# Two spreadings of a norm's inverse roots sent through memory, and two weight differences ordered behind a multiplication, in an encoder layer

## The chip, the cores and the metric

The kernel runs on one core of a Trainium2 chip. A core has a matrix engine (TensorE, PE in the profile; its weight loads are PEld), three engines for elementwise work (VectorE or DVE, ScalarE or ACT, GpSimd or POOL), and SyncE (SP), which here only issues DMAs. ScalarE issues DMAs too. Each engine carries out its own instructions strictly in the order in which they stand in its queue; an instruction whose operand isn't there stops everything behind it on that engine. TensorE writes to PSUM banks of 128 x 512 numbers; VectorE and ScalarE read these and the main on-chip memory (SBUF). DRAM is reached by DMA alone.

The metric is the time of one execution on the device in microseconds (us), lower is better.

## The reference

An encoder layer on 1024 tokens of width 1024, in float32. One RMSNorm feeds a projection; its columns go to two kinds of attention (A, a sliding window; B, a neighbourhood on a grid), each with 512 output columns and an RMSNorm of its own; one output projection; an RMSNorm and a gated MLP with 2816 inner columns; a last RMSNorm.

```python
def rmsnorm(x, g):
    y = x * lax.rsqrt(jnp.mean(x * x, axis=-1, keepdims=True) + EPS)
    return y * g
...
mix = jnp.concatenate([rmsnorm(o_a, norm_a[l]), rmsnorm(o_b, norm_b[l])], axis=-1)
h = h + jnp.einsum('bse,ed->bsd', mix, w_out[l])
hn = rmsnorm(h, norm_ffn[l])
h = h + conv_gated_mlp(hn, w_gate[l], w_up[l], conv_w[l], conv_b[l], w_down[l])
return rmsnorm(h, norm_final)
```

The change is in the two norms on the second and the fourth of these lines: that of attention B and that of the MLP.

## The kernel before

**Layout.** Activations lie transposed: the 128 partitions hold columns of the model, the tokens run along a row. A tile is 128 x 1024, and each is worked on in two halves of 512 tokens (h = 0 and 1). Every matrix product is made of three matmuls for each pair of blocks: operands and weights are split into a high part (ScalarE copies with rounding) and a low part (VectorE subtracts), and high x high, high x low and low x high are added up in a PSUM bank (`block`, L179 to L181, and `group`, L1043 to L1045).

**A norm.** Since a token is a column here, its sum of squares runs over partitions. `inverse_narrow` transposes the accumulated squares on TensorE (L217), VectorE reduces them to `v`, 128 partitions x 4 numbers, one for each of 512 tokens (L219), ScalarE takes the root (L220), VectorE the reciprocal (L229). These carry a high priority. `widen` then spreads `v` again: four transposes on TensorE (L236), each of one column of `v` taken 128 times, so that a PSUM bank holds each token's inverse root in all 128 partitions (tile `sw`). VectorE multiplies an activation tile by the norm's gain and by this bank in one instruction.

The second half of the last norm does it in another way (`as_rows`, L1497 and on): one transpose turns `v` into 4 rows of 128, ScalarE copies them to SBUF, a DMA writes these 2 KB to DRAM (`spread`), and a second DMA reads them back into all 128 partitions, 256 KB (`wide`). Both DMAs are issued by SyncE.

**Order.** TensorE's order is the program's own. For the other engines a planner sorts the instructions by their place in the program, their priority (`tc.high_priority`) and by when it believes their operands to be there; `behind("name")` forbids it to put what is inside ahead of a named instruction. Queues of DMAs are sorted like the engine that issues them.

**The stage.** Near 350 us the last attention units end. `vb2` holds the roots of attention B's norm for both halves. For each half the kernel spreads the root (`widen`), multiplies four tiles (L996) and splits them (L997 ScalarE, L998 VectorE) to `mg[4:8]`. Between the halves the first two output weights are begun (`load_wo`, L979 to L983) and three blocks of the A half of the output projection are run (`fill(3)`).

Then comes the B half of the output projection, for h = 0 and 1 and d = 0 to 7, four blocks of three matmuls each; every result is added to the residual (L1063), written to DRAM (`h1d`, issued by ScalarE, L1064), squared (L1067) and added up (L1069). The MLP norm's first half falls into h = 1: its `v` is made behind d = 1 and spread within d = 3, behind the second block. `normed(0, ...)` then multiplies tiles 0 to 3 and later 4 to 7 (L1074), and `operand` splits them (L1050, L1051) for the first gate products `p1` and `p2` (tiles `x` and `z`). During `p2` the second half's squares are transposed, and behind it its `v` is spread.

**The weight differences.** The gate and up products use a scheme of seven products in place of eight, which needs sums and differences of weight blocks and of operands. `head_weights(i, "s2")` makes such a difference of weights for each of the four first units (i = 0 to 3): it loads half a weight tile (L1037) and subtracts it from a sum made before (`sub`, L1083; as `ws<-ws,raw` in the profile). It stands late in the program, behind `normed(1, ...)`, but the planner can move it forward. Half tiles share three raw buffers.

Of the kernel before, what the change touches and what calls it, by code (L numbers as in the profile page):

```python
# [13 lines left out]
F32 = mybir.dt.float32  # L14
F32R = mybir.dt.float32r
AF = mybir.ActivationFunctionType
ALU = mybir.AluOpType
PSUM = bass.MemoryType.PSUM

D, S, HD = 1024, 1024, 64  # L20
KT = D // 128
NB = S // 128
HALF = 512
# [29 lines left out]
C_NMIX, C_NFFN, C_NFIN, C_NA, C_NB, C_CW, C_CB, C_SINK = 0, 8, 16, 24, 28, 32, 98, 120  # L53
# [5 lines left out]
def hybrid_layer(tc, xT, w_first, w_in, w_out, w_gate, w_up, w_down, small, sink, rpb, consts, rope, out):  # L59
    nc = tc.nc  # L60
    with ExitStack() as ctx:
# [7 lines left out]
        tpool = inner("temps", 3)  # L69
        apool = inner("att", 2)  # L70
        spool = inner("stats", 6)

        slots = {"xg": 16, "op": 14, "mix": 8, "rstd": 1}

        def big(name, tag, dt=F32):
            return lpool.tile([128, S], dt, name=name, tag=tag, bufs=slots[tag])
# [4 lines left out]
        def bank(name, tag):  # L81
            return psum.tile([128, HALF], F32, name=name, tag=tag)
# [7 lines left out]
        col = lambda c: par[:, c:c + 1]  # L90
# [15 lines left out]
        for name, dst, n in (("h", his, 2), ("h", his, 2), ("l", los, 2), ("l", los, 2), ("w", None, 2)):  # L106
            t = flat(big(name, "mix", F32R)[:, :], n)
# [26 lines left out]
        ident = cst[:, K_ID:K_ID + 128]  # L134
# [17 lines left out]
        mark = {}  # L152

        def behind(*names):

            stack = ExitStack()
            for n in names:
                stack.enter_context(tc.issue_after(mark[n].ins))
            return stack
# [51 lines left out]
        def inverse_narrow(sqs, dim, tag, n=4):  # L211

            ps = bank("ss", tag)
            v = cpool.tile([128, n], F32, name="v4", tag="v4", bufs=4, padded_shape=[128, 4])
            if len(sqs) == 1:
                for c in range(n):
                    nc.tensor.transpose(ps[:, c * 128:(c + 1) * 128], sqs[0][:, c * 128:(c + 1) * 128], ident)  # L217
                with tc.high_priority(offset=500):
                    nc.vector.tensor_reduce(v, ps[:, 0:n * 128].rearrange("p (c w) -> p c w", w=128), axis=mybir.AxisListType.X, op=ALU.add)  # L219
                    mark["narrow root"] = nc.scalar.activation(v, v, AF.Sqrt, bias=eps, scale=1.0 / dim)  # L220
            else:
                for i, sq in enumerate(sqs):
                    for c in range(n):
                        nc.tensor.matmul(ps[:, c:c + 1], sq[:, c * 128:(c + 1) * 128], ones[:, 0:1], start=c == 0 and i == 0,
                                         stop=i == len(sqs) - 1, skip_group_check=True)
                with tc.high_priority(offset=500):
                    nc.scalar.activation(v[:, 0:n], ps[:, 0:n], AF.Sqrt, bias=eps, scale=float(D) / dim)
            with tc.high_priority(offset=500):
                mark["narrow"] = nc.vector.reciprocal(v[:, 0:n], v[:, 0:n])  # L229
            return v  # L230

        def widen(v, tag, n=4):

            wide = bank("sw", tag)
            for c in range(n):
                nc.tensor.transpose(wide[:, c * 128:(c + 1) * 128], v[:, c:c + 1].to_broadcast([128, 128]), ident)  # L236
            return wide
# [427 lines left out]
        xg, first = [None] * KT, [Project(m) for m in range(3)]  # L665
# [58 lines left out]
        t = quarters(big("f", "mix"))  # L724
# [140 lines left out]
        def fill(n):  # L865
            while n > 0 and next(filler, False):
                n -= 1
# [3 lines left out]
        for g in range(2):  # L871
            for b in range(NB):
                q, t = unit_window(g, b)
# [59 lines left out]
        for u in range(len(flat)):  # L933
            q, t, need, kind = flat[u]
# [42 lines left out]
        def load_wo(d, early):  # L977
            raw = wpool.tile([128, 4, 128], F32, name="raw", tag="raw", bufs=2) if early else half_raw()
            nc.sync.dma_start(raw, w_out[d, :, 4:8, :])  # L979
            t = big("wo", "op", F32R)[:, :].rearrange("p (s j c) -> p s j c", s=2, c=128)  # L980
            with behind("narrow", "narrow root"):
                nc.scalar.activation(t[:, 0], raw, AF.Copy)
                nc.vector.tensor_tensor(t[:, 1], raw, f32(t[:, 0]), op=ALU.subtract)  # L983
            return [(t[:, 0, j, :], t[:, 1, j, :]) for j in range(4)]

        fill(6)
        with tc.high_priority(offset=500):
            vb2 = [inverse_narrow([last[:, tsl(h)]], 512, "pt") for h in range(2)]
        fill(4)
        mg[4:8] = [(big("mgh", "xg", F32R), big("mgl", "xg", F32R)) for _ in range(4)]  # L990
        for h in range(2):
            wide = widen(vb2[h], "pt")
            for i in range(4):
                x = mix[4 + i][:, tsl(h)]
                hi, lo = (t[:, tsl(h)] for t in mg[4 + i])
                nc.vector.scalar_tensor_tensor(x, x, col(C_NB + i), wide, op0=ALU.mult, op1=ALU.mult)  # L996
                nc.scalar.activation(hi, x, AF.Copy)  # L997
                nc.vector.tensor_tensor(lo, x, f32(hi), op=ALU.subtract)  # L998
            if h == 0:
                wo = [load_wo(d, True) for d in range(2)]  # L1000
                fill(3)
# [10 lines left out]
        def split_w(src, n):  # L1012

            pad = [128, 4, 128]
            hi = fpool.tile([128, n, 128], F32R, name="whi", tag="wh", bufs=9, padded_shape=pad)
            lo = fpool.tile([128, n, 128], F32R, name="wlo", tag="wl", bufs=9, padded_shape=pad)
            nc.scalar.activation(hi, src, AF.Copy)  # L1017
            nc.vector.tensor_tensor(lo, src, f32(hi[:, :, :]), op=ALU.subtract)  # L1018
            return [(hi[:, j, :], lo[:, j, :]) for j in range(n)]

        def load_raw(src, n):
            raw = fpool.tile([128, n, 128], F32, name="raw", tag="raw", bufs=3, padded_shape=[128, KT, 128])
            nc.sync.dma_start(raw, src)
            return raw
# [9 lines left out]
        def load_half(src):  # L1034

            t = half_raw()
            nc.sync.dma_start(t, src)  # L1037
            return t
# [16 lines left out]
        K1, K2 = range(0, 4), range(4, 8)  # L1055
        B, W = {}, {}
        late, total = [], [None, None]
        at = lambda k, h: h1[k][:, tsl(h)]
# [12 lines left out]

        def normed(h, wide, ds):
            for d in ds:
                nc.vector.scalar_tensor_tensor(at(d, h), at(d, h), col(C_NFFN + d), wide, op0=ALU.mult, op1=ALU.mult)  # L1074

        def pure(f):
            raw = load_raw(w_gate[f], KT)
# [5 lines left out]
        sub = lambda o, x, y: nc.vector.tensor_tensor(o, x, y, op=ALU.subtract)  # L1083
# [5 lines left out]
        def head_weights(i, name):  # L1089
            f, t = FO[i], wsum[i]  # L1090
            if name == "s1":
                u = load_raw(w_up[f], KT)
                nc.vector.tensor_tensor(t, u[:, 0:4], u[:, 4:8], op=ALU.add)
            elif name == "s2":
                g = load_half(w_gate[f, :, 0:4])
                sub(t, t, g)
            elif name == "s4":
                g = load_half(w_gate[f, :, 4:8])
                sub(t, g, t)
            elif name == "s3":  # L1100
                g, u = load_half(w_gate[f, :, 0:4]), load_half(w_up[f, :, 0:4])
                sub(t, g, u)
            else:
                t = load_half(w_up[f, :, 4:8])
            W[f, name] = split_w(t, 4)

        for h in range(2):
            for d in range(KT):
                if h == 0 and d + 2 < KT:
                    wo.append(load_wo(d + 2, False))  # L1110
                ps = bank("pj", ("o", "s", "pj")[(h * KT + d) % 3])
                for step, _ in enumerate(product(ps, wo[d], mg[4:8], h)):
                    if (h, d, step) == (1, 3, 1):
                        wide = widen(v, "pt")
                late.append((d, h, ps))
                if h == 1 and d == 1:
                    v = inverse_narrow([total[0]], D, "pt")
                settle_out()
                if h == 0 and d in (3, 4):
                    pure((0, FT // 2)[d - 3])  # L1120
                if h == 0 and d >= 5 or h == 1 and d == 0:
                    head_weights((d - 5) % KT, "s1")
                if h == 1 and d == 3:
                    normed(0, wide, K1)
                    B[1, 1] = [operand(at(k, 0), "xg") for k in K1]
                if h == 1 and d == 4:
                    normed(0, wide, K2)
                    B[2, 1] = [operand(at(k, 0), "xg") for k in K2]
# [146 lines left out]
        v = inverse_narrow([total[1]], D, "pt")  # L1275
        units[1].p2()
        wide = widen(v, "pt")
# [270 lines left out]
        for i, (p, j, c) in enumerate(order):  # L1548
# [10 lines left out]
            ps = banks[p, j]  # L1559
# [27 lines left out]
        for k, cols in enumerate(quarters):  # L1587
            for j in (2, 3):
                ps = banks[6, j]
# [17 lines left out]
        first = quarters[1].start  # L1607
# [98 lines left out]
```

## Time and profile before

| | |
|---|---|
| median of 3 runs | 1014.76 us |
| lowest and highest | 1014.33 and 1014.77 us |
| the profiled execution | 1014.52 us |
| its span, first to last instruction | 1012.7 us |
| mean granted TensorE clock | 0.998 |
| matmuls | 5083 |

The profiled execution is 1.8 us longer than its span and 0.24 us below the median. Rows of a timeline give the start, the duration (of the whole group, where several alike are merged, with their count at the end), engine, line, operation, output and inputs, and in brackets the idle time before with what ended it. A matmul of 512 columns is shown with 0.38 us, but is pipelined: the next one starts 0.22 us later. An operation of VectorE on 128 x 512 is shown with 0.68, and the next starts 0.60 later. `SPq` and `ACTq` are DMA issues by SyncE and ScalarE.

The instructions of the two spreadings, from the answers on the tile `sw`: L236 takes 0.27 us for one transpose, L996 and L1074 take 0.74 us for one tile's half. The MLP norm's multiplications run from 393.9 to 425.2 us for both halves together, attention B's from 352.6 to 363.3.

### The profile page before, as it was taken

The numbers are of one execution on the slowest core, as the hardware profiler recorded it, in microseconds if no ns is written. First come the engines' busy times: TensorE is split into PE (matmuls) and PEld (weight loads), VectorE is DVE, ScalarE is ACT, GpSimd is POOL, SyncE is SP. The second block draws the span as 40 slices with busy tenths as digits, with TensorE's granted clock in tenths as the row PEclk, the third lists the DMA queues.
The fourth block names the chain that finished last, engine by engine and source line by source line (L and its number), as shares of the span: only waits on it lengthen the run. The fifth ranks groups of instructions, "written<-read, shape, count | busy, mean of one in ns | idle before, by whom it ended". The sixth has DMA issues, their size and how long they took to land.

```text
span 1012.7 us, 14836 instructions
## 1 busy us (share of the span) xinstructions
PE 1005.1 (99%) x5083; PEld 889.5 (88%) x5083; DVE 835.0 (82%) x1570; ACT 560.7 (55%) x1079; POOL 101.9 (10%) x186
## 2 busy tenths in 40 slices
PE   9999999999999999999999999999999999999997
PEld 8899998999899888888888888888888888888887
DVE  7899887768888799999987786786777678996775
ACT  8468776658687554565544443444444645544451
POOL 0224342232232100000000000000000000000001
PEclk9999999999999999999999999999999999999999
DMA  8223122333334366232552333323232699866654
GB/s 295 83 76 92 32 73 63 84 84 84 83 94 136 126 203 222 74 103 64 200 185 92 107 115 115 105 94 119 100 127 84 236 333 318 305 233 238 213 168 177
DMA packets 68372, 145.20 MB, mean 143 GB/s; under 512 B 8260, under 2 KB 18760, under 8 KB 68296
## 3 DMA queue, kind: packets, MB, share of 16 engines
q1 hardware_dynamic: 58216, 119.01, 36.6%
q10 hardware_dynamic: 10080, 25.24, 6.4%
q8 instruction: 40, 0.66, 0.3%
q14 instruction: 36, 0.29, 0.1%
HBM read 103.85 MB, written 28.58 MB: 131 GB/s over the span
## 4 chain that ended last, share of the span: by engine, by line
PE 96%; ACT 1%; DVE 1%; DMA 1%; SPq 0%; issue 0%; DVEq 0%
PE pj L179 8%; PE pj L181 8%; PE pj L180 8%; PE x L1045 8%; PE x L1043 8%; PE x L1044 7%; PE dn L1045 7%; PE dn L1044 7%; PE dn L1043 7%; PE s L393 4%; PE y L1045 4%; PE y L1043 4%; PE y L1044 4%; PE pt L548 2%; PE pt L472 2%; PE z L1043 2%
## 5 line engine op out<-in xcount | busy, mean ns | idle before, releaser
L1043 PE MATMUL x<-hg,whi 128*128 128x512 f32 x352 | 133.5, 379 | 0.0
L1044 PE MATMUL x<-hg,whi 128*128 128x512 f32 x352 | 133.4, 379 | 0.0
L1045 PE MATMUL x<-hg,wlo 128*128 128x512 f32 x352 | 133.4, 379 | 0.0
L1043 PE MATMUL dn<-xd,whi 128*128 128x512 f32 (+1 forms) x330 | 120.8, 366 | 0.0
L1044 PE MATMUL dn<-xd,whi 128*128 128x512 f32 (+1 forms) x330 | 120.5, 365 | 0.0
L1045 PE MATMUL dn<-xd,wlo 128*128 128x512 f32 (+1 forms) x330 | 120.5, 365 | 0.0
L1017 ACT ACTIVATE whi<-ws 128x512 fp32r<-128x512 f32 (+1 forms) x100 | 60.8, 621 | 75.2 <-DVE ws L1157 14.5
L432 ACT ACTIVATE p<-p,nm 128x385 f32<-128x385 f32 (+3 forms) x128 | 75.0, 586 | 45.9 <-DVE nm L424 43.5
L179 PE MATMUL pj<-xgh,whi 128*128 128x512 f32 x245 | 99.7, 407 | 0.0
L436 POOL TENSOR_SCALAR p<-p,sm 128x384 f32<-128x384 f32 (+1 forms) x128 | 75.9, 606 | 195.2 <-DVE sm L434 178.1
L180 PE MATMUL pj<-xgl,whi 128*128 128x512 f32 x245 | 92.9, 379 | 0.0
L181 PE MATMUL pj<-xgh,wlo 128*128 128x512 f32 x245 | 92.9, 379 | 0.0
L1017 ACT ACTIVATE whi<-raw 128x512 fp32r<-128x512 f32 (+1 forms) x102 | 61.0, 611 | 49.9 <-PE x L1044 15.0
L1018 DVE TENSOR_TENSOR wlo<-ws,whi 128x512 fp32r<-128x512 f32 (+1 forms) x100 | 66.7, 680 | 20.0 <-ACT whi L1017 19.7
L447 DVE TENSOR_TENSOR pl<-pt,ph 128x384 fp32r<-128x384 f32 (+2 forms) x108 | 63.4, 587 | 17.1 <-ACT ph L446 16.0
L1043 PEld LDWEIGHTS x<-hg,whi 128*128 128x128 f32 x352 | 66.5, 189 | 9.4
L1044 PEld LDWEIGHTS x<-hg,whi 128*128 128x128 f32 x352 | 66.5, 189 | 9.4
L1045 PEld LDWEIGHTS x<-hg,wlo 128*128 128x128 f32 x352 | 66.5, 189 | 9.4
L1018 DVE TENSOR_TENSOR wlo<-raw,whi 128x512 fp32r<-128x512 f32 (+1 forms) x102 | 66.5, 668 | 5.8 <-ACT whi L1017 5.8
L1518 POOL TENSOR_TENSOR h<-h,wide 128x256 f32<-128x256 f32 x4 | 2.8, 731 | 671.3 <-ACT wide L1514 671.3
L446 ACT ACTIVATE ph<-pt 128x384 fp32r<-128x384 f32 (+2 forms) x108 | 55.3, 512 | 25.7 <-PE pt L472 14.5
L1043 PEld LDWEIGHTS dn<-xd,whi 128*128 128x128 f32 x330 | 62.5, 189 | 7.8
(273 smaller groups left out, 2505.3 us busy)
## 6 DMA issues: line engine op xcount, KB each, us to landing
xd<-x SPq DMA_DIRECT2D x77, 256.0 KB, 4.9
raw<-in_w_down_dram SPq DMA_DIRECT2D x72, 256.0 KB, 4.6
raw<-in_w_gate_dram SPq DMA_DIRECT2D x22, 512.0 KB, 3.5
raw<-in_w_up_dram SPq DMA_DIRECT2D x22, 512.0 KB, 3.7
x<-c ACTq DMA_DIRECT2D x22, 512.0 KB, 2.8
raw<-in_w_in_dram SPq DMA_DIRECT2D x30, 256.0 KB, 2.7
raw<-in_w_down_dram SPq DMA_DIRECT2D x36, 192.0 KB, 4.4
x<-t ACTq DMA_DIRECT2D x11, 512.0 KB, 2.6
```

The source lines that it names most:

```text
L179: nc.tensor.matmul(ps, w[0], mv(x[0][:, tsl(h)]), start=first, stop=False)
L180: nc.tensor.matmul(ps, w[0], mv(x[1][:, tsl(h)]), start=False, stop=False)
L181: nc.tensor.matmul(ps, w[1], mv(x[0][:, tsl(h)]), start=False, stop=last)
L432: nc.scalar.activation(p[:, j, 0:e], p[:, j, 0:e], AF.Exp, bias=nm, scale=-1.0, accum_out=sm[:, j:j + 1])
L436: mark["scaled"] = nc.gpsimd.tensor_scalar(p[:, i, 0:m], p[:, i, 0:m], sm[:, i:i + 1], 1.0, op0=ALU.mult, op1=ALU.mult)
L446: mark["high"] = nc.scalar.activation(ph[:, 0:n], ps[:, 0:n], AF.Copy)
L447: mark["rest"] = nc.vector.tensor_tensor(pl[:, 0:n], ps[:, 0:n], f32(ph[:, 0:n]), op=ALU.subtract)
L1017: nc.scalar.activation(hi, src, AF.Copy)
L1018: nc.vector.tensor_tensor(lo, src, f32(hi[:, :, :]), op=ALU.subtract)
L1043: nc.tensor.matmul(ps, w[0], x[0], start=first and i == 0, stop=False, skip_group_check=True)
L1044: nc.tensor.matmul(ps, w[0], x[1], start=False, stop=False, skip_group_check=True)
L1045: nc.tensor.matmul(ps, w[1], x[0], start=False, stop=last and i == len(ws) - 1, skip_group_check=True)
```

## The change

A new helper `by_rows` does what `as_rows` does, with a place for the rows and for the result that the caller gives, a DRAM tile of its own, ScalarE as issuer of the write, and a choice of who issues the read.

1. Attention B's norm, second half: `by_rows` in place of `widen`, right behind the first half's `widen`, ahead of that half's multiplications and of `fill(3)`. The read is issued by SyncE. Rows and result lie in a new tile `rstdb`.
2. The MLP norm's first half: `by_rows` in place of `widen`, behind the last block of d = 2 in place of the second block of d = 3. ScalarE issues the read. Rows and result lie in the same tile.
3. The differences `s2` of the units 2 and 3 may not be put ahead of the fourth multiplication of the MLP norm's first half.

```diff
+        roots_pool = ctx.enter_context(tc.tile_pool(name="roots", bufs=1, space=bass.MemoryType.DRAM))
+
+        def by_rows(v, rows, wide, tag, read):
+            ps, roots = bank("row", tag), roots_pool.tile([4, 128], F32, name="roots")
+            nc.tensor.transpose(ps[0:4, 0:128], v, ident)
+            with tc.high_priority(offset=500):
+                nc.scalar.activation(rows, ps[0:4, 0:128], AF.Copy)
+                nc.scalar.dma_start(roots, rows)
+                read.dma_start(wide, bass.AP(tensor=roots.tensor, offset=roots.offset, ap=[[0, 128], [1, HALF]]))
...
+        rstd = big("rstdb", "rstd")
         for h in range(2):
-            wide = widen(vb2[h], "pt")
+            if h == 0:
+                wide = widen(vb2[0], "pt")
+                by_rows(vb2[1], rstd[0:4, HALF:HALF + 128], rstd[:, 0:HALF], "pt", nc.sync)
+            else:
+                wide = rstd[:, 0:HALF]
...
             for d in ds:
-                nc.vector.scalar_tensor_tensor(at(d, h), at(d, h), col(C_NFFN + d), wide, op0=ALU.mult, op1=ALU.mult)
+                mark["normed"] = nc.vector.scalar_tensor_tensor(at(d, h), at(d, h), col(C_NFFN + d), wide, op0=ALU.mult, op1=ALU.mult)
+                if (h, d) == (0, K1[-1]):
+                    mark["first normed"] = mark["normed"]
...
                 g = load_half(w_gate[f, :, 0:4])
-                sub(t, t, g)
+                with behind(*["first normed"] * (i > 1)):
+                    sub(t, t, g)
...
                 for step, _ in enumerate(product(ps, wo[d], mg[4:8], h)):
-                    if (h, d, step) == (1, 3, 1):
-                        wide = widen(v, "pt")
+                    if (h, d, step) == (1, 2, 3):
+                        wide = rstd
+                        by_rows(v, wide[0:4, 0:128], wide[:, HALF:S], "pt", nc.scalar)
+                        wide = wide[:, HALF:S]
```

## The prediction

> **What bounds the kernel now.** I read the page's totals first, then what TensorE waited for, then the timeline of TensorE alone, and only then the other engines in the two places that the change touches.
>
> ```profile
> span 1012.7 us, 14836 instructions
> ...
> PE 1005.1 (99%) x5083; PEld 889.5 (88%) x5083; DVE 835.0 (82%) x1570; ACT 560.7 (55%) x1079; POOL 101.9 (10%) x186
> ...
> PEld sw L236 <- DVE v L229: 0.3, 1, 0.3
> ```
>
> The third line is from the list of waits between 385 and 416 us, and it is the only one of TensorE there. So in this stretch the time goes down by exactly as much work as TensorE loses, as long as no operand comes later than it is wanted; and one operand, the root v of the MLP norm's second half, is already just late. A gain can't exceed the TensorE work removed plus that wait. I price that work first.
>
> ```profile
> 391.47 0.60 PE L236 MATMUL sw<-cst,v 128*128 128x128 f32 x4
> 391.82 0.46 PE L179 MATMUL pj<-mgh,wo 128*128 128x512 f32 x1
> 392.12 0.38 PE L180 MATMUL pj<-mgl,wo 128*128 128x512 f32 x1
> ```
>
> This is one spreading (four transposes of v's columns) and the two matmuls behind it. The same place of the last norm, which already goes through memory:
>
> ```profile
> 986.92 0.38 PE L1045 MATMUL dn<-xd,wlo 128*128 128x512 f32 x1
> 987.14 0.27 PE L1499 MATMUL row<-cst,v 128*4 128x128 f32 x1
> 987.16 0.46 PE L1043 MATMUL dn<-xd,whi 128*128 128x512 f32 x1
> 987.46 0.38 PE L1044 MATMUL dn<-xd,whi 128*128 128x512 f32 x1
> ```
>
> Without a norm between them matmuls start 987.14 - 986.92 = 0.22 us apart. Four transposes push the second matmul behind them from 391.47 + 0.22 = 391.69 to 392.12: 0.43 us. One row transpose pushes it from 987.14 + 0.22 = 987.36 to 987.46: 0.10 us. **Each spreading replaced saves TensorE 0.33 us, the two of them 0.66 us.** A gain of 0.66 us is 0.07% of 1012.7; 0.2% of the run is 2.0 us, about what a measurement of this kernel can tell from no change.
>
> **The attention norm's second half.** Removed: four transposes; added: one transpose, one small ScalarE copy, a write of 2 KB issued by ScalarE, a broadcast read of 256 KB issued by SyncE. Their durations stand in the last norm's rows:
>
> ```profile
> 987.45 0.27 ACT L1501 ACTIVATE rows<-row 4x128 f32<-4x128 f32 x1 [2.76 <-PE row L1499]
> ...
> 987.74 0.33 SPq L1502 DMA_DIRECT2D spread<-rows  x1
> ...
> 988.92 0.35 SPq L1503 DMA_DIRECT2D wide<-spread  x1
> ...
> 991.94 1.41 DVE L1520 SCALAR_TENSOR_TENSOR h<-h,par,wide 128x512 f32<-128x512 f32 x2 [0.47 <-DMA wide<-spread]
> ```
>
> From the row transpose (987.14) to the first multiplication with the spread root (991.94) it is 4.80 us: 0.60 to the write, 1.18 until it has landed and the read goes out, 3.02 for the read. In the new order the row transpose stands right behind the first half's spreading:
>
> ```profile
> 351.95 0.60 PE L236 MATMUL sw<-cst,v 128*128 128x128 f32 x4
> ...
> 357.57 1.40 DVE L996 SCALAR_TENSOR_TENSOR mixb<-mixb,par,sw 128x512 f32<-128x512 f32 x2
> ...
> 365.77 0.68 DVE L983 TENSOR_TENSOR wo<-raw,wo 128x512 fp32r<-128x512 f32 x1
> ...
> 366.86 0.38 PE L181 MATMUL pj<-mgh,wo 128*128 128x512 f32 x1
> ...
> 353.00:358.00 5.00, 5.00 (x26) 4.37 (x26) 5.00 (x9) 1.90 (x3) 0.00 (x0) 1.00 0.03 11
> ```
>
> The four transposes take 391.82 - 391.47 = 0.35, so the row stands at 351.95 + 0.35 = 352.30 and the root is spread at 357.10. The second half's first multiplication is the second of the pair at 357.57, so about 358.2: 1.1 us to spare. The last row (columns: TensorE, its loads, VectorE, ScalarE, GpSimd, clock, share of the DMA engines, GB/s) has the DMA engines 0.03 busy from 353 to 358; nothing delays the two transfers, and neither queue has work behind them that is wanted sooner: ScalarE runs 1.90 us of these 5. The cover is thin further on. VectorE is full all through those 5 us, and its low part of the third output weight ends at 365.77 + 0.68 = 366.45, for a matmul at 366.86: 0.41 us, of which the faster TensorE takes 0.33. If the spread root came x late, x - 1.1 - 0.08 would be lost, at most the 0.33 and then more. I take the full saving, 0.33 us, with bounds of 0 and 0.33. The multiplication itself costs VectorE the same with the root in the other memory (1.41 for two above, 1.40 for two here).
>
> **The MLP norm's first half.** The row transpose moves ahead by six matmuls, from 391.47 to 391.47 - 6 x 0.22 = 390.15, and with the first saving to 389.82. What is there by then:
>
> ```profile
> 388.68 0.33 ACTq L1064 DMA_DIRECT2D h1d<-h  x1
> ...
> 389.15 0.17 DVE L229 RECIPROCAL v<-v 128x4 f32<-128x4 f32 x1
> ...
> 390.42 0.68 DVE L1063 TENSOR_TENSOR h<-pj,h 128x512 f32<-128x512 f32 x1
> 392.08 1.35 DVE L1083 TENSOR_TENSOR ws<-ws,raw 128x512 f32<-128x512 f32 x2 [0.98 <-DMA raw<-in_w_gate_dram]
> 393.35 0.68 DVE L1069 TENSOR_TENSOR s<-s,s 128x512 f32<-128x512 f32 x1
> 393.95 1.40 DVE L1074 SCALAR_TENSOR_TENSOR h<-h,par,sw 128x512 f32<-128x512 f32 x2
> ```
>
> v is ready at 389.15 + 0.17 = 389.32, half a microsecond ahead: TensorE doesn't wait for it. The spread root comes at 389.82 + 4.80 = **394.62** if the transfers are as quick as in the last norm. VectorE began the multiplications at 393.95. Between these it has one addition (0.60 in a full row of them) that TensorE has released by then, so 394.55 is when it first sits idle: 0.1 us late at best. At worst the transfers queue:
>
> ```profile
> h1d<-h ACTq DMA_DIRECT2D x7, 256.0 KB, 4.3
> raw<-in_w_gate_dram SPq DMA_DIRECT2D x4, 256.0 KB, 5.3
> ...
> 389.00:391.00 2.00, 2.00 (x11) 1.76 (x10) 2.00 (x5) 0.00 (x0) 0.00 (x0) 1.00 0.88 301
> 391.00:392.00 1.00, 1.00 (x8) 0.87 (x8) 0.10 (x1) 0.63 (x1) 0.00 (x0) 1.00 0.36 139
> ...
> 987.00:992.00 5.00, 5.00 (x38) 4.63 (x37) 1.44 (x3) 1.62 (x3) 0.00 (x0) 1.00 0.15 53
> ```
>
> The spill of 388.68 is ahead of the write on ScalarE's queue; with the median of its kind (4.3) it lands at 392.98 instead of the write's 389.82 + 0.60 + 1.18 = 391.60, 1.4 us later. The read, with the 5.3 of a load of its size in that window for 3.0, takes 2.3 more: 398.3, 3.7 us late. The share of the DMA engines falls from 0.88 to 0.36 just when the write would land (it was 0.15 in the last norm), so I take a value near the quick end, **0.6 us late**.
>
> The Trainium skill speaks against this placing: "DMA: Bandwidth & Descriptors", section "Latency and other measured facts", gives an HBM access 0.2 us on average and 2 us at high load, and a smaller fixed cost where the load is lighter. As an estimate from that page two transfers under load would be 3.6 us longer than two in quiet; by it the root comes at 398.2, and the time is that of rival (b) below. No run here shows a round trip under load.
>
> The second read is issued by ScalarE itself, so ScalarE stands still until the write has landed, 1.2 us or more. Behind it stand the squares of the output tiles and their spills, then the high parts of the normed operands, which can't begin before the multiplications anyway; ScalarE is busy 0.63 of the us from 391 and not at all in the two before. That costs nothing unless the write takes over 2 us.
>
> **What VectorE's lateness costs.** From 392.08 on VectorE has no idle time until the second root is out, and TensorE meets it twice:
>
> ```profile
> 407.62 2.50 DVE L1051 TENSOR_TENSOR hg<-h,hg 128x512 fp32r<-128x512 f32 x4
> ...
> 408.96 0.38 PE L1044 MATMUL z<-hg,whi 128*128 128x512 f32 x1
> ...
> 411.24 1.29 DVE L1083 TENSOR_TENSOR ws<-ws,raw 128x512 f32<-128x512 f32 x2
> ...
> 411.33 0.60 PE L217 MATMUL ss<-cst,s 128*128 128x128 f32 x4
> ...
> 413.04 0.68 DVE L219 TENSOR_REDUCE v<-ss 128x4 f32<-128x512 f32 x1
> ...
> 414.24 0.17 DVE L229 RECIPROCAL v<-v 128x4 f32<-128x4 f32 x1
> ...
> 414.15 0.38 PE L1045 MATMUL z<-hg,wlo 128*128 128x512 f32 x1
> ...
> 414.47 0.65 PE L236 MATMUL sw<-cst,v 128*128 128x128 f32 x4
> ```
>
> The fifth operand's low part ends at 407.62 + 0.68 = 408.30 for a matmul at 408.96: 0.66 us to spare, all of which the faster TensorE uses up. The spreading of the second half's v stands at 414.47, 0.10 behind 414.15 + 0.22, because v ends at 414.41. To keep the 0.66, v has to come 0.56 us sooner. It can: its transposes end at 411.33 + 0.60 = 411.93, the reduction starts at 413.04, 1.1 us later, behind two weight differences (1.2) and one other operation.
>
> **The two weight differences** are those at 411.24 already, behind the multiplications; the new order forbids only that they fill the longer gap at 394, where their data (loaded after the first pair's) would stall VectorE. Alone that costs nothing; its work is the same 1.29 us. What matters is whether they still stand ahead of the reduction. If the multiplications come later and the second half's sums of squares earlier, the reduction, which has a high priority, meets the differences while they are still undone and goes ahead of one or both. That gives v 0.6 to 1.2 us back, against the 0.6 lost to the later root: net 0 to -0.6 for v, and so for TensorE.
>
> **The sum.** -0.66 for TensorE's work, +0.3 for what VectorE's order takes back (the middle between keeping all and none): **-0.36 us**, 1014.52 for the profiled execution to 1014.16, and 1014.76 to 1014.4 for the median, which stands 0.24 above the profiled one. From -0.66 (1014.1) to 0 (1014.8).
>
> **Rivals.** (a) *The late root is paid at the second half's spreading, slower.* VectorE keeps its order; 0.6 to 1.9 us of waiting for the first half's root (part of the queueing above) goes through its full row to v at 414.41, and TensorE waits there. It decides as soon as the root is over 0.1 us late and the differences stay ahead of the reduction. For it: no idle time to absorb anything from 392.08 to 414.24. Against: the reduction is free to move. Time 1014.76 + 0.9 = 1015.7, from 1015.3 to 1016.7. (b) *The round trip queues in full*, 2.0 to 3.7 us late by the spill ahead and the loads beside it, with the same consequence: 1016.8 to 1018.5. For it the 0.88 ahead of the write; against it the 0.36 behind. (c) *The gain doesn't arrive*: v comes when it came, TensorE merely waits 0.66 us longer at 414.47: 1014.7 to 1014.9. For it the 0.10 that it waits already. (d) A gain over 2 us would need a stall of TensorE that the timeline doesn't have.
>
> **How the numbers follow.** Forecast 0.45, (a) 0.32, (b) 0.11, (c) 0.10, (d) 0.02. Faster by over 0.2% is (d) alone, 0.02; slower is (b), 0.11; the rest, 0.87, lies within 0.2%. The likeliest case's own range is 1014.1 to 1014.8. The range reaches from 1013.9, a run's scatter of 0.2 below the full saving, to 1016.7, the end of (a), and leaves out (b) and (d).
>
> **What would show it.** Two row transposes with the next matmuls 0.10 instead of 0.43 us late. The first read landing before 358.2 on the old clock and no wait of VectorE there. The first multiplication of the MLP norm at 394.6 to 395.5, with a wait for the read ahead of it: later than 396.5 is (b). Then the order at v: a reduction ahead of the two differences is the forecast, behind them (a). The spreading at 414.47 moves by the net of the whole change, since TensorE keeps its pace after it. The forecast is wrong if TensorE shows a wait at the first matmuls of z, or at the output weights near 366.

## The result

The changed kernel takes 1016.17 us (median of 20 runs, 1015.39 to 1017.88), the one before 1014.76 (median of 20): a ratio of 1.0016, with a 95% interval from 1.0010 to 1.0022. It is 1.4 us slower. The profiled execution took 1016.52 us, its span is 1014.7.

From the page of the changed kernel and its list of TensorE's waits:

```profile
span 1014.7 us, 14832 instructions
...
PE z L1059 <- DVE hg L1066: 1.5, 1, 1.5
...
PE x L1059 <- DVE hg L1066: 0.3, 1, 0.3
```

Both waits are new: TensorE stands at matmuls of `x` and `z` for the low parts of the MLP norm's operands. In its own timeline the wait at `z` is the hole between these rows:

```profile
408.92 0.38 PE L1058 MATMUL z<-hg,whi 128*128 128x512 f32 x1
410.80 0.48 PE L1059 MATMUL z<-hg,whi 128*128 128x512 f32 x1 [1.50 <-DVE hg L1066]
```

The next matmul should have come 0.22 us after 408.92; it came 1.88 after. What VectorE was late for stands on ScalarE's queue (timeline of ScalarE, with its DMA issues) and in VectorE's own row:

```profile
388.60 0.33 ACTq L1079 DMA_DIRECT2D h1d<-h  x1
390.41 0.27 ACT L78 ACTIVATE rstdb<-row 4x128 f32<-4x128 f32 x1 [1.52 <-PE row L76]
390.71 0.27 ACTq L79 DMA_DIRECT2D roots<-rstdb  x1
...
391.07 0.33 ACTq L1079 DMA_DIRECT2D h1d<-h  x1
393.32 0.33 ACTq L80 DMA_DIRECT2D rstdb<-roots  x1
```

```profile
393.65 0.68 DVE L1078 TENSOR_TENSOR h<-pj,h 128x512 f32<-128x512 f32 x1
395.03 0.69 DVE L1084 TENSOR_TENSOR s<-s,s 128x512 f32<-128x512 f32 x1 [0.70 <-ACT s L1082]
397.55 0.75 DVE L1089 SCALAR_TENSOR_TENSOR h<-h,par,rstdb 128x512 f32<-128x512 f32 x1 [1.82 <-DMA rstdb<-roots]
...
410.06 2.49 DVE L1066 TENSOR_TENSOR hg<-h,hg 128x512 fp32r<-128x512 f32 x4
...
414.88 0.68 DVE L229 TENSOR_REDUCE v<-ss 128x4 f32<-128x512 f32 x1
...
416.07 0.17 DVE L239 RECIPROCAL v<-v 128x4 f32<-128x4 f32 x1
416.16 0.66 DVE L1100 TENSOR_TENSOR ws<-ws,raw 128x512 f32<-128x512 f32 x1
```

The row transpose and its copy came when they were expected. Then the write needed 393.32 - 390.71 = 2.61 us until the read could go out (1.18 in the last norm), and the read 397.55 - 393.32 = 4.23 us (3.02 there). The first multiplication began at 397.55 in place of 393.95, 3.60 us later. VectorE filled the gap with one residual addition and one sum of squares (0.60 each) and otherwise stood still.

From there on VectorE's row is full as before, but shorter by those two operations. The low parts that `z` waits for (the group at 410.06) begin 2.44 us later than before (407.62). TensorE had 0.66 us to spare there before, and it reaches its second matmul of `z` 1.84 us later (410.80, 408.96 before). That is where the loss arises: at the first matmul of `z` the changed kernel is only 0.18 us behind (408.92, 408.74 before), and 0.17 of this was there ahead of the change (352.12 and 351.95).

The second half's `v` comes 1.83 us later: 416.07 - 397.55 = 18.52 us instead of 414.24 - 393.95 = 20.29, since one weight difference now stands behind the reciprocal too (416.16). TensorE's spreading of it is late by what `z` has cost already:

```profile
352.12 0.60 PE L246 MATMUL sw<-cst,v 128*128 128x128 f32 x4
352.55 0.27 PE L76 MATMUL row<-cst,v 128*4 128x128 f32 x1
352.58 0.46 PE L189 MATMUL pj<-mgh,whi 128*128 128x512 f32 x1
352.88 0.38 PE L190 MATMUL pj<-mgl,whi 128*128 128x512 f32 x1
...
416.09 0.38 PE L1060 MATMUL z<-hg,wlo 128*128 128x512 f32 x1
416.31 0.64 PE L246 MATMUL sw<-cst,v 128*128 128x128 f32 x4
```

414.47 before, 416.31 now: +1.84 us, as at `z`, and 0.22 us behind the matmul ahead of it, so that `v` adds no wait. TensorE's saving of 0.66 us was used up ahead of `z`, most of it at `x`. This execution is 0.35 us above its kernel's median; a root that came a little sooner would explain the median's 1.4 us, but no trace of such a run was kept.

### The profile page after: what moved, and what is told of

Read it like the earlier page. It is cut to its first block, busy times and chain, and to the rows that moved or that the text cites. A ratio compares the mean times of both kernels' runs of the same rounds, so it can differ in the third digit from the quotient of the medians.

```text
span 1014.7 us, 14832 instructions
## 1 busy us (share of the span) xinstructions
PE 1004.9 (99%) x5077; PEld 887.4 (87%) x5077; DVE 835.1 (82%) x1570; ACT 560.8 (55%) x1081; POOL 101.4 (10%) x186
## 4 chain that ended last, share of the span: by engine, by line
PE 94%; DVE 2%; DMA 1%; ACT 1%; SPq 0%; issue 0%; DVEq 0%
PE pj L189 8%; PE pj L191 7%; PE pj L190 7%; PE x L1058 7%; PE x L1060 7%; PE x L1059 7%; PE dn L1060 7%; PE dn L1058 7%; PE dn L1059 7%; PE s L403 4%; PE y L1060 4%; PE y L1059 4%; PE y L1058 4%; PE z L1059 2%; PE pt L558 2%; PE pt L482 2%
## 5 line engine op out<-in xcount | busy, mean ns | idle before, releaser
L1394 ACT ACTIVATE xd<-xd 128x512 fp32r<-128x512 f32 x77 | 47.2, 625 | 40.5 <-DMA xd<-x 40.4
```

## The experiments

The theory after the result: **the MLP root's round trip is late because of the traffic around it**, and everything else follows from VectorE's row. Rivals: A, the attention half disturbs VectorE's full row; O, the planner's new order of VectorE's work costs the time; Q, the round trip is that slow in itself; S, ScalarE's standing still ahead of the read is what costs.

Ratios are to the kernel before, with 95% intervals. "Write" is the time from its issue to the read's issue, "first" the start of the first multiplication of the MLP norm; both are of the one profiled execution, the medians of all runs. The runs of the kernel before beside the experiments had medians of 1014.72 and 1014.73 us.

| run | median us | ratio | write us | first |
|---|---|---|---|---|
| before | 1014.76 | 1 | | 393.95 |
| the change | 1016.17 | 1.0016 (1.0010 to 1.0022) | 2.6 | 397.55 |
| e1_attention_only | 1014.38 | 0.9997 (0.9988 to 1.0006) | | |
| e2_mlp_only | 1015.63 | 1.0015 (1.0006 to 1.0024) | 1.2 | 397.00 |
| e3_no_order | 1016.87 | 1.0023 (1.0014 to 1.0032) | 1.5 | 397.90 |
| e4_both_roots | 1014.73 | 1.0001 (0.9992 to 1.0010) | 3.3 | 395.72 |
| e5_spills_behind | 1015.07 | 1.0004 (0.9995 to 1.0012) | 1.2 | 396.00 |
| e6_loads_behind | 1016.25 | 1.0013 (1.0005 to 1.0022) | 3.0 | 397.45 |
| e7_all_behind | 1014.51 | 0.9999 (0.9990 to 1.0008) | 1.2 | 395.45 |
| e8_read_sync | 1016.72 | 1.0023 (1.0014 to 1.0032) | | 398.60 |
| e10_early | 1018.09 | 1.0033 (1.0021 to 1.0046) | 4.7 | 399.24 |
| e12_third_weight | 1015.22 | 1.0004 (0.9995 to 1.0013) | 1.7 | 396.58 |
| e13_first_spill | 1015.70 | 1.0010 (1.0001 to 1.0019) | 1.2 | 397.16 |
| e14_second_spill | 1016.60 | 1.0015 (1.0006 to 1.0024) | 1.7 | 397.29 |

In two rows "write" holds more than the write. A DMA counts as landed here at the last update of its semaphore in the trace: by that the write took 4.4 us in e10 and 1.2 in e12, and the read was held up on ScalarE's queue by work ahead of it. In e8, where SyncE reads, the write took 1.6. The profiled executions of e4 (1016.13) and e8 (1017.57) lie 1.4 and 0.85 us above their medians, that of e14 (1015.95) 0.65 below: their traces show what can happen, not the usual run.

### Which part of the change

**The attention half alone.** The MLP norm's `by_rows` is `widen` behind the second block of d = 3 again, and the differences are free.

> The attention norm's half goes through memory, the MLP norm's first half is spread on TensorE as before, and no order is set for the weight differences. Theory (the MLP root's round trip through memory is late): nothing is late here, three transposes less, 0.3 us faster than before, about 1014.4. Rival A (the attention half's root disturbs VectorE's full row up to the output weights): slower than before, up to 1016. Rival O (the order of the weight differences and the reduction costs the time): like the theory, 1014.4.

1014.38, 0.4 below the runs of before beside it; the interval takes in no change. Rival A is out: the loss isn't here. The thin cover that the prediction named did show, at the low part of the third output weight (timeline of TensorE):

```profile
366.47 0.38 PE L190 MATMUL pj<-mgl,wo 128*128 128x512 f32 x1
367.09 0.48 PE L191 MATMUL pj<-mgh,wo 128*128 128x512 f32 x1 [0.24 <-DVE wo L993]
```

The second row is 0.40 us late. In this execution the spread root itself came 0.42 us late: the first multiplication waits for the read until 358.89. So the 0.33 us that the row transpose saves are spent again here, and about 0.1 comes back at the second MLP spreading, where TensorE now finds v ready.

**The MLP half alone.**

> Only the MLP norm's first half goes through memory, with the weight differences held as in the change; the attention half is as before. Theory: all of the loss is here, about 0.3 us more than the changed kernel, 1016.5; the first multiplication 3 us behind where its operands else allow it. Rival A: 1014.5 to 1014.8. Rival O: as the theory in time, but with the multiplications begun on time.

1015.63: the loss is here. It is smaller than expected (1016.5), though its interval overlaps that of the change. In the profiled execution the write took 1.2 us only, but the read 4.8, so that the root came at 397.00 all the same.

**The differences left to the planner.**

```diff
-                with behind(*["first normed"] * (i > 1)):
-                    sub(t, t, g)
+                sub(t, t, g)
```

> The changed kernel with the planner free to place the weight differences of units 2 and 3. Theory: their data land near 397, so if the planner puts them into the gap ahead of the multiplications the first of these begins near 398.7 instead of 397.5 and the time is 0.7 to 1.2 us above the changed kernel, 1016.9 to 1017.4; if it leaves them, the same 1016.2. Rival O: faster than the changed kernel, towards 1014.8.

The planner does put one of the two ahead of the multiplications, where it waits for its load (VectorE):

```profile
397.29 0.69 DVE L1100 TENSOR_TENSOR ws<-ws,raw 128x512 f32<-128x512 f32 x1 [1.47 <-DMA raw<-in_w_gate_dram]
397.90 0.75 DVE L1089 SCALAR_TENSOR_TENSOR h<-h,par,rstdb 128x512 f32<-128x512 f32 x1
```

By the trace the read had landed at 396.36; it was the difference that held the multiplication until 397.90. 1016.87 is 0.7 above the changed kernel, but the two intervals overlap: that the third part of the change is worth something, because of the gap that the second part makes, is what this trace suggests and the times don't settle. Rival O is out for the differences: leaving them free gains nothing.

**Both ways at once.** The row transpose, the write, the read and the order stay, but the multiplications read a bank spread on TensorE as before.

> The changed kernel, but the MLP norm's first half is also spread on TensorE behind the second block of d = 3, as before, and the multiplications read that bank; the row transpose, the write, the read and the held differences stay, and nothing waits for the read. Theory: the loss goes, since nothing waits for the round trip: 1014.76 - 0.33 + 0.10 = 1014.5. Rival O, or ScalarE standing still ahead of the read, or traffic of the read itself as the cause: 1015.5 to 1016.2 stays.

1014.73, 1.4 below the changed kernel, with everything of the change still there but VectorE's wait for the read, and four transposes more on TensorE. **That shows the wait for the root to be the loss**, and neither the two transfers' traffic, nor the order, nor ScalarE's standing still. The 0.2 above the 1014.5 expected are within the interval. The profiled execution is the slowest of the eleven runs: the write took 3.3 us, and VectorE's first two differences waited 1.9 us for their loads (1.0 before), so that the multiplications began at 395.72, without a wait for the read. It shows another way to be late, and the median carries the argument.

### What makes the root late

**The spills behind the read.** The spills of d = 1 (ahead of the write on ScalarE's queue) and of d = 2 (between write and read) go behind the read:

```diff
-            nc.scalar.dma_start(spilled[d][:, tsl(h)], at(d, h))
+            spill = lambda: nc.scalar.dma_start(spilled[d][:, tsl(h)], at(d, h))
+            if (d, h) == (1, 1):
+                held.append(spill)
+            else:
+                with behind(*["read"] * ((d, h) == (2, 1))):
+                    spill()
...
                         wide = wide[:, HALF:S]
+                        with behind("read"):
+                            held.pop()()
```

> The changed kernel, with the spills of the tiles d = 1 and d = 2 (256 KB each, ScalarE's queue) issued behind the MLP root's read instead of ahead of its write and its read. Theory (the round trip queues behind and beside other traffic): the write lands in 1.2 to 1.6 us instead of 2.6, the first multiplication starts near 396 instead of 397.5, the time is about 1015.3. Rival Q (the round trip is that slow in itself, whatever is on the queues): 397.5 and 1016.2 stay.

Write 1.2, read 3.1, first multiplication at 396.00, 1015.07: a little better than expected, and 1.1 below the changed kernel. By the trace the root had landed at 395.39, and a sum of squares stood ahead of the multiplication. Rival Q is out.

**The loads behind the read.** The loads for the differences 2 and 3 are issued by ScalarE behind the read.

> The changed kernel, with the two loads for the weight differences of units 2 and 3 (256 KB each) issued by ScalarE behind the MLP root's read instead of by SyncE beside it. Theory: the read takes 3.0 to 3.5 us instead of 4.2, the first multiplication starts near 396.5, the time is about 1015.4. Rival Q: no change, 1016.2.

No gain, 1016.25: a miss. With the spills still ahead the write took 3.0 us and the read 4.0, and the root came at 397.45. Taking the loads away alone shows no gain.

**Both.**

> Both of these: the two spills and the two loads behind the read. Theory: write 1.2 to 1.6 us, read 3.0, the first multiplication near 395, TensorE waits at z 0.3 us or less, the time 1014.6 to 1015.0. Rival Q: 1016.2.

1014.51, at the quick end of what was expected. Write and read on ScalarE's queue, then the first multiplication and the region of the second `v` on VectorE:

```profile
390.85 0.27 ACTq L79 DMA_DIRECT2D roots<-rstdb  x1
...
392.05 0.33 ACTq L80 DMA_DIRECT2D rstdb<-roots  x1
392.40 0.46 ACTq L1079 DMA_DIRECT2D h1d<-h  x1
```

```profile
394.78 0.69 DVE L1089 TENSOR_TENSOR s<-s,s 128x512 f32<-128x512 f32 x1 [0.70 <-ACT s L1087]
395.45 0.75 DVE L1094 SCALAR_TENSOR_TENSOR h<-h,par,rstdb 128x512 f32<-128x512 f32 x1
...
413.99 0.16 DVE L239 RECIPROCAL v<-v 128x4 f32<-128x4 f32 x1
414.07 0.66 DVE L1105 TENSOR_TENSOR ws<-ws,raw 128x512 f32<-128x512 f32 x1
```

The multiplication follows the sum of squares without a listed wait for the DMA: by the trace the read landed at 395.43, just in time. It still starts 1.5 us behind the kernel before, but v comes at 413.99 instead of 414.24, since two operations were done ahead of it and one difference behind it, and no wait of a matmul is listed in the stage. This is the prediction's forecast, reached only with the traffic out of the way. Below the kernel before by 0.2 us, it isn't told apart from it.

**One spill at a time.**

> The changed kernel with only the spill of d = 1 (the one ahead of the root's write on ScalarE's queue) moved behind the read; the spill of d = 2 stays between write and read. Theory: the write lands in 1.2 us as in the run with both spills moved, but the read still has 256 KB ahead of it and takes 4 to 4.8 us; the first multiplication near 396.5, time about 1015.6. If the write's delay is the whole cause: 395.5 to 396 and 1015.1, as with both.

> The changed kernel with only the spill of d = 2 moved behind the read; the spill of d = 1 stays ahead of the write. Theory: the write takes 2.6 us as in the changed kernel, the read 3.0 to 3.5; the first multiplication near 396.7, time about 1015.7. If the first spill's place ahead of the write is the whole cause: no gain, 1016.2.

1015.70 and 1016.60, roots at 397.16 and 397.29. The issues from the dma view of both, between 392 and 398 us (KB each, median us from issue to landing), first the run with the spill of d = 1 moved, then that with the spill of d = 2 moved, then that with both:

```profile
rstdb<-roots ACTq DMA_DIRECT2D x1, 256.0 KB, 4.7
```

```profile
rstdb<-roots ACTq DMA_DIRECT2D x1, 256.0 KB, 4.5
```

```profile
rstdb<-roots ACTq DMA_DIRECT2D x1, 256.0 KB, 3.1
```

With the spill of d = 1 moved the write is quick (1.2), as expected, and the read isn't. With the spill of d = 2 moved the write is slower (1.7), and the read takes 4.5 us, against the expectation of 3.0 to 3.5. Each spill by itself is enough for a root near 397.2 in these executions, which both took 1015.9; they don't show where the 0.9 us between the medians comes from.

The spill of d = 1 is still under way at the read's issue in the second of these runs: issued at 388.96, it takes 4.4 us, and the read goes out at 392.73 (dma view from 388.5 to 389.5):

```profile
h1d<-h ACTq DMA_DIRECT2D x1, 256.0 KB, 4.4
```

That fits all twelve traces with a round trip at the MLP norm. In the three in which no spill was under way at the read's issue (e5, e7, e12) the read took 3.1 to 3.4 us until it had landed; in the nine others a spill landed 0.2 to 1.9 us behind that issue, and the read took 3.7 to 4.7. This is a match over the runs and was not tried by itself.

**Who issues the read.**

```diff
-                        by_rows(v, wide[0:4, 0:128], wide[:, HALF:S], "pt", nc.scalar)
+                        by_rows(v, wide[0:4, 0:128], wide[:, HALF:S], "pt", nc.sync)
```

> The changed kernel with the MLP root's read issued by SyncE; in its queue it stands behind the first of the two loads that come free at 393. ScalarE no longer stands still for the write. Theory: what delays the root is traffic, not who waits for it: the read goes out at 393.6 and lands near 397.5 to 398, time 1016 to 1016.5. Rival S (ScalarE's wait for the write is what costs the time): 1015.2 or less.

1016.72, the root at 398.60. SyncE's queue shows why it is later still:

```profile
394.15 0.33 SPq L1052 DMA_DIRECT2D raw<-in_w_gate_dram  x1
394.57 0.38 SPq L80 DMA_DIRECT2D rstdb<-roots  x1
```

The read stands behind a load which waits for its buffer; the write had landed at 392.97, 1.6 us earlier. ScalarE no longer waits, and nothing is gained. But with a later root this run can't price ScalarE's standing still by itself; rival S is out by e4, where ScalarE stands for the write as before and the loss is gone.

### Two attempts at a better kernel

**Starting sooner.** The sums are transposed within d = 1 and the row behind the first block of d = 2.

> The changed kernel with the MLP norm's first sums transposed within d = 1 (behind its second block) instead of behind d = 1, and the row transpose behind the first block of d = 2 instead of its fourth: the round trip starts 1.9 us sooner. Theory: the first multiplication comes 1 to 1.9 us sooner, at 395.6 to 396.5, less if the engines' full load up to 391 holds the write back all the same; TensorE's wait at z falls by the same; time 1014.6 to 1015.3. Rival O (the planner's order of VectorE costs the time): no gain, 1016.

1018.09, the slowest of all: a plain miss. The write went out at 389.86, but right behind a spill of 389.36 and into engines that were 0.84 busy from 389 to 392; by the trace it landed at 394.25, 0.2 us behind that spill. The read followed at 394.53 and took 4.7. It had stood on ScalarE's queue behind the squares and the spill of d = 2, for a tile that VectorE was late with, as VectorE had itself waited for a load (VectorE, then ScalarE):

```profile
392.78 0.69 DVE L1100 TENSOR_TENSOR ws<-ws,raw 128x512 f32<-128x512 f32 x1 [2.01 <-DMA raw<-in_w_gate_dram]
393.39 0.68 DVE L1078 TENSOR_TENSOR h<-pj,h 128x512 f32<-128x512 f32 x1
```

```profile
394.10 0.63 ACT L1082 ACTIVATE s<-h 128x512 f32<-128x512 f32 x1 [4.27 <-DVE h L1078]
394.11 0.33 ACTq L1079 DMA_DIRECT2D h1d<-h  x1
394.53 0.39 ACTq L80 DMA_DIRECT2D rstdb<-roots  x1
```

So even a quick write could not have sent the read out much sooner in this order. TensorE lost 0.4 us at the row transpose too, for a v that it now reached too soon.

**The third output weight.** From the kernel with all four transfers behind the read; two low parts of the attention half go behind that of the weight.

> The kernel with two spills and two loads behind the read (1014.5), and in the attention stage the low parts of the last two tiles of the second half ordered behind the low part of the third output weight, so that this one comes 0.6 us sooner. Theory: TensorE's wait near 366 (0.2 to 0.3 us) goes, TensorE keeps 0.6 of the 0.66 us, time 1014.1 to 1014.3, faster than both kernels. If VectorE's row is what sets the end all the same: 1014.5.

1015.22. The wait near 366 is gone, as meant, but VectorE's later work now comes in another order, and TensorE found another wait:

```profile
390.88 0.17 DVE L239 RECIPROCAL v<-v 128x4 f32<-128x4 f32 x1
...
PE row L76 <- DVE v L239: 1.0, 1, 1.0
```

v came at 391.05 for a row transpose that was due 1.0 us before. Why `v` came so late wasn't followed further. No version was measured that is faster than the kernel before beyond its interval.

## Why the prediction was wrong

The forecast was 1014.4 and a small gain; the result is a loss of 1.4 us, of the other sign. That it lies inside the range, which the prediction drew to the end of rival (a), is luck: the root was later than (a) had it. Two steps failed, both about the MLP norm's first half: how late its root comes (0.6 us reckoned, 3.0 measured), and where this lateness is paid (at `v` in the sum, at `z` in the trace).

- **TensorE's saving, 0.66 us: right.** The matmul two behind the new row transpose stands at 352.88; behind four transposes alone it would stand 0.65 us after their start (391.47 and 392.12 before), at 352.77. That is 0.11 us for the row, as in the last norm.
- **The attention half, 0.33 us kept: not shown.** Write, read and first multiplication of the changed kernel:

```profile
353.16 0.52 ACTq L79 DMA_DIRECT2D roots<-rstdb  x1
...
355.42 0.33 SPq L80 DMA_DIRECT2D rstdb<-roots  x1
...
358.48 0.75 DVE L1011 SCALAR_TENSOR_TENSOR mixb<-mixb,par,rstdb 128x512 f32<-128x512 f32 x1
```

  The read took 3.06 us as reckoned, the write 2.26 instead of 1.18, so that the root came just in time and not 1.1 us ahead; in nine of the eleven experiments with this half VectorE is listed as waiting 0.2 to 0.4 us for it. The write took 2.2 to 2.4 us in every one of these traces, with the DMA engines 0.05 busy from 353 to 355.5 in the changed kernel: traffic doesn't explain that, and what does stays open. The cover at the third output weight turned out as thin as computed, and took the saving back in e1's execution; its median, 0.35 us below the kernel before, isn't told apart from it.
- **The MLP root "0.6 us late": this step failed.** Against the 394.55 from which VectorE was reckoned idle the root was 3.0 us late, near the far bound of 3.7. The two terms that were too small are the write, 2.61 us for 1.18, and the read, 4.23 for 3.02. I chose the quick end because the DMA engines' share falls to 0.36 when the write lands. The write was late all the same, and I looked at the wrong window for the read: it runs from 393 to 397, when the trace of before already showed the engines busy again, 0.46 over the four us and 0.70 from 394 to 396. The row of these two us, and that of the changed kernel:

```profile
394.00:396.00 2.00, 2.00 (x11) 1.74 (x10) 2.00 (x5) 1.25 (x3) 0.00 (x0) 1.00 0.70 222
```

```profile
393.50:397.50 4.00, 4.00 (x20) 3.52 (x19) 1.53 (x3) 0.63 (x1) 0.00 (x0) 1.00 0.68 202
```

  The last two columns are the engines' share and GB/s. The Trainium skill's rule that was weighed ("DMA: Bandwidth & Descriptors", "Latency and other measured facts": dearer under load) pointed the right way: its estimate of 3.6 us more for both transfers stands against 2.64 measured (2.61 + 4.23 for 1.18 + 3.02).
- **Where the lateness is paid: this step failed too.** The sum took it into account at `v` alone. But the prediction had found that the faster TensorE uses up all the 0.66 us to spare at `z`, and the low parts for `z` stand ahead of the two differences, so that their moving can't help there. By its own rows a root 0.6 us late makes these low parts 0.6 us later (the multiplications 1.2, less one addition done ahead), and TensorE waits 0.6 us at `z`: nearly all of the gain was gone already. Measured, the low parts came 2.44 us later, and TensorE stood there 1.50 us.
- **The order at v: right.** One of the two differences did move behind the reduction. That kept `v` from adding to the loss; it could not take back what `z` had cost.
- **The rivals.** The mechanism is that of (b), the queueing ahead of and beside the round trip (e5, e7), but at the price of (a), and paid at `z`, which the prediction names as a sign of being wrong and prices nowhere. (b) was reckoned as if the whole lateness reached TensorE; of 3.60 us VectorE made up 1.16 by two operations done in the gap, and 0.66 was to spare.
- **ScalarE's standing still "costs nothing unless the write takes over 2 us":** the write took 2.6, and e4, where ScalarE still stands for it, shows no loss.

## What to carry to other kernels

A round trip through memory has two windows, and each has to be looked up in the stage where it will run: the engines' share when the write lands, and the share and the issues beside it when the read runs. Where a spill that nobody waits for is issued just ahead on the same queue, put it behind the read before judging the idea. And when one engine's row is full for 20 us, a wait at its start is a wait for everyone behind it, less what the engine can do meanwhile and less what that reader has to spare: follow it to each reader in turn, and not to the last one only.

## What the runs showed of the hardware

At the MLP norm the write of 2 KB landed 1.2 us after its issue in all four traces in which the spill of d = 1 was out of its way (e5, e7, e12, e13). In the eight with that spill ahead of it on ScalarE's queue it took 1.2 us (e2), 1.5 (e3), 1.6 (e8, e14), 2.6 (the change), 3.0 (e6), 3.3 (e4) and 4.4 (e10); in the last four of these runs it landed 0.2 to 0.4 us behind that spill. So with traffic about, one profile of such a transfer is a sample and no price. A quiet stage is no price either: at the attention norm the same kind of write took 2.2 to 2.4 us in every trace. The runs of the changed kernel scatter over 2.5 us (1015.39 to 1017.88) against 1.6 before (1014.33 to 1015.93); whether the write's scatter is the cause isn't shown.
